# RMSNorm with SiLU: six load buffers as parts of one tile, and four early block loads as two transfers of 64 KB runs

## The chip, the cores and the metric

The kernel runs on one core of one Trainium2 chip. The metric is the device time of one execution in microseconds (us); lower is better. The times shown are medians of several runs; profiles are of one execution each.

## The reference

The input `x` has 8 x 1024 rows of 2048 float32 numbers, `gamma` 2048 numbers, `eps` is 1e-5:

```python
rms = np.sqrt(np.mean(x ** 2, axis=-1, keepdims=True) + eps)
out = gamma * x / rms
return (out * (1 / (1 + np.exp(-out)))).astype(np.float32)
```

Each row is divided by its root mean square, multiplied by gamma, and put through SiLU. 67.1 MB are read and 67.1 MB are written.

## The kernel before, in words

The 8192 rows are cut into 16 blocks of 512 rows. A block is a tile `xt` of 128 partitions, each holding `J = 4` whole rows that lie next to each other in memory: 32 KB per partition, 4.19 MB per block. The pool has six buffers (`BUFS`), so at most six blocks are on the chip, and block b + 6 takes the buffer of block b after that block has been stored. All of the work is done in place.

What each engine does for a block:

- ACT's queue issues the load (`load`, L52 to L55). The queue is also the one that feeds ScalarE with its work, in program order.
- The squares of the four rows are summed, some on ScalarE (`squares_scalar`, L60 to L69, into column j of `ss`), the rest on VectorE (`squares_vector`, L71 to L75). `share(b)` (L77) is the number of rows for ScalarE: 2, or 1 for even blocks from 4 to 12.
- ScalarE takes the root (`root`, L82), VectorE the reciprocal (`invert`, L87), then VectorE multiplies each row by its reciprocal and by gamma (`multiply`, L92, four instructions of 128 x 2048).
- ScalarE applies SiLU in two halves of two rows each (`silu`, L98), and SyncE's queue issues the store (`store`, L102). SyncE issues nothing else apart from gamma's load.
- ScalarE needs another function table for the root than for SiLU: a table load (ACT_TABLE_LOAD, 1.28 us) stands ahead of each root and ahead of the SiLU that follows.

The order on each engine is the order of the program, written out by hand (`manual_schedule`). Loads 0 and 1 are issued at the beginning. Gamma (one row) is copied to all partitions by eight matmuls; ScalarE then copies one element of the result (L116), so that loads 2 to 5 (L117, L118) are issued only after gamma is in place. After that `load(b + 3)` is issued within `squares_scalar(b + 1)`, just after the first square of block b + 1 (L67 to L69), and it waits for the store of the block that had its buffer.

For b below `SOON = 3` and for the last two, a step is: multiply(b), squares_scalar(b + 1), silu(b) with store(b), squares_vector(b + 1), root(b + 1). In between it is: squares_scalar(b + 1), squares_vector(b + 1), root(b + 1), multiply(b), silu(b) with store(b). Then invert(b + 1) follows. The last block is multiplied by gamma alone, and its reciprocal goes into SiLU as a scale, row by row (L152 to L159).

Of the kernel before, what the change touches and what calls it, by code (L numbers as in the profile page):

```python
# [1 line left out]

# [4 lines left out]

ACT = mybir.ActivationFunctionType
ALU = mybir.AluOpType


@with_exitstack
def kernel(
    ctx: ExitStack,
    tc: tile.TileContext,
    x: bass.AP,
    gamma: bass.AP,
    eps: bass.AP,
    out: bass.AP,
):  # L20

    nc = tc.nc
    P = nc.NUM_PARTITIONS
    f32 = mybir.dt.float32
    x2 = x.flatten_outer_dims()
    o2 = out.flatten_outer_dims()  # L30
    n, d = x2.shape
    J = 4
    BUFS = 6
    nblk = n // (P * J)
    xb = x2.rearrange("(b p j) d -> b p (j d)", p=P, j=J)
    ob = o2.rearrange("(b p j) d -> b p (j d)", p=P, j=J)

    singles = ctx.enter_context(tc.tile_pool(name="singles", bufs=1))
    pool = ctx.enter_context(tc.tile_pool(name="pool", bufs=BUFS))
    small = ctx.enter_context(tc.tile_pool(name="small", bufs=2))  # L40
    psum = ctx.enter_context(tc.tile_pool(name="psum", bufs=1, space=bass.MemoryType.PSUM))

    Q = 4
    w = d // Q
    g = singles.tile([P, d], f32)
    eps_t = singles.tile([P, 1], f32)
    ones = singles.tile([P, P], f32)
    junk_a = psum.tile([P, d], f32, name="junk_a")
    junk_v = psum.tile([P, d], f32, name="junk_v")
    blocks, sss, rmss, rstds = {}, {}, {}, {}  # L50

    def load(b):  # L52
        xt = pool.tile([P, J * d], f32, name="xt")
        nc.scalar.dma_start(out=xt, in_=xb[b])  # L54
        blocks[b] = xt  # L55

    def row(b, j):
        return blocks[b][:, j * d:(j + 1) * d]

    def squares_scalar(b, loads=()):  # L60


        sss[b] = small.tile([P, J], f32, name="ss")
        for j in range(share(b)):
            nc.scalar.activation(out=junk_a, in_=row(b, j), func=ACT.Square,  # L65
                                 accum_out=sss[b][:, j:j + 1])
            if j == 0:  # L67
                for s in loads:
                    load(s)  # L69

    def squares_vector(b):  # L71
        for j in range(share(b), J):
            nc.vector.tensor_tensor_reduce(  # L73
                out=junk_v, in0=row(b, j), in1=row(b, j), scale=1.0, scalar=0.0,
                op0=ALU.mult, op1=ALU.add, accum_out=sss[b][:, j:j + 1])  # L75

    def share(b):  # L77
        return 1 if 4 <= b <= 12 and b % 2 == 0 else 2

    def root(b):  # L80
        rms = small.tile([P, J], f32, name="rms")
        nc.scalar.activation(out=rms, in_=sss.pop(b), func=ACT.Sqrt, scale=1.0 / d, bias=eps_t)  # L82
        rmss[b] = rms

    def invert(b):
        rstd = small.tile([P, J], f32, name="rstd")
        nc.vector.reciprocal(out=rstd, in_=rmss.pop(b))  # L87
        rstds[b] = rstd

    def multiply(b):  # L90
        for j in range(J):
            nc.vector.scalar_tensor_tensor(out=row(b, j), in0=row(b, j), scalar=rstds[b][:, j:j + 1],  # L92
                                           in1=g, op0=ALU.mult, op1=ALU.mult)

    def silu(b):
        for h in range(0, J, 2):
            cols = slice(h * d, (h + 2) * d)
            nc.scalar.activation(out=blocks[b][:, cols], in_=blocks[b][:, cols], func=ACT.Silu)  # L98
        store(b)

    def store(b):
        nc.sync.dma_start(out=ob[b], in_=blocks[b])  # L102

    with tc.manual_schedule():

        load(0)
        nc.vector.memset(ones, 1.0)  # L107
        nc.vector.memset(eps_t, float(eps))
        nc.scalar.activation(out=junk_a[:, 0:1], in_=ones[:, 0:1], func=ACT.Square)  # L109
        nc.sync.dma_start(out=g[0:1, :], in_=bass.AP(tensor=gamma.tensor, offset=gamma.offset, ap=[[d, 1], [1, d]]))  # L110
        for c in range(Q):
            cols = slice(c * w, (c + 1) * w)
            nc.tensor.matmul(junk_v[:, cols], ones[0:1, :], g[0:1, cols], start=True, stop=True)  # L113
        load(1)
        nc.vector.tensor_copy(out=g, in_=junk_v)  # L115
        nc.scalar.copy(out=junk_a[:, 0:1], in_=junk_v[:, d - 1:d])  # L116
        for b in range(2, BUFS):  # L117
            load(b)  # L118

        last = nblk - 1
        SOON = 3
        squares_scalar(0)
        squares_vector(0)
        root(0)
        invert(0)
        for b in range(last):
            loads = [b + 3] if BUFS <= b + 3 < nblk else []
            if b < SOON:  # L130
                multiply(b)
                squares_scalar(b + 1, loads)
                silu(b)
                squares_vector(b + 1)
                root(b + 1)
            elif b < last - 1:
                squares_scalar(b + 1, loads)
                squares_vector(b + 1)
                root(b + 1)
                multiply(b)  # L140
                silu(b)
            else:
                multiply(b)
                squares_scalar(b + 1)
                silu(b)
                squares_vector(b + 1)
                root(b + 1)
            if b + 1 < last:
                invert(b + 1)


        for j in range(J):  # L152
            if j == J // 2:
                invert(last)
            nc.vector.tensor_mul(out=row(last, j), in0=row(last, j), in1=g)  # L155
        for j in range(J):
            nc.scalar.activation(out=row(last, j), in_=row(last, j), func=ACT.Silu,  # L157
                                 scale=rstds[last][:, j:j + 1])
        store(last)  # L159


# [1 line left out]
_INS = ['x', 'gamma', 'eps']  # L163
_OUTS = [((8, 1024, 2048), 'float32')]

_NUMBERS = {'eps': 9.999999747378752e-06}


# [26 lines left out]
```

## Time and profile before

| What | Value |
|---|---|
| time, median of 3 runs | 317.02 us (316.7 to 317.08) |
| span of the profiled execution, first to last instruction | 315.1 us (the page gives no time around it; 1.9 us below the median of the runs) |
| VectorE busy | 235.3 us, 75% |
| ScalarE busy | 213.9 us, 68% |
| TensorE busy | 7.2 us, 2% |
| DMA | 134.24 MB, mean 426 GB/s |
| loads | 16 of 4096 KB, median 38.7 us from issue to landing |
| stores | 16 of 4096 KB, median 29.0 us from issue to landing |

How to read it. The page cuts the span into 40 equal slices and gives each engine's busy share of a slice in tenths; DMA is the mean over the core's 16 DMA engines, and the row below it is what they moved in GB/s. A packet is one contiguous run that one DMA engine moves: here 32 KB, a partition's share of a block. A transfer has landed when all of its packets are done and its semaphore has been raised. Loads go through ACT's queue and stores through SyncE's; both are served by the same 16 DMA engines. A line such as "66.72 38.05 DMA xt<-in_x_dram" of the chain of waits is a piece of the chain that ended last: start, length, and what it was. In the timeline an entry has start, length, engine, line, operation, output and inputs, and in brackets how long the engine was idle before and what ended it.

### The profile page before, as it was taken

Reading aid. Unit: us, or ns where it says so; the run is one execution under the profiler, and the core shown is the slowest. Engines: PE = TensorE matmul, PEld = TensorE weight load, DVE = VectorE, ACT = ScalarE, POOL = GpSimd, SP = SyncE. Lnnn points to the kernel's source line nnn. Section 1 sums busy time; section 2 is a strip of 40 time slices with the busy share of each in tenths; the row PEclk is TensorE's granted clock in tenths of the full one; section 3 lists DMA queues with packets and bytes.
Section 4 is the critical chain, followed back from the end, with each engine's and each line's share of the span. In section 5 each row is a group of like instructions: output and inputs, shape, how many; then the busy total and the mean of one; then the engine's idle time right before and its main releaser. Section 6 shows DMA issues by size and latency. Waiting matters only on the chain.

```text
span 315.1 us, 439 instructions
## 1 busy us (share of the span) xinstructions
PE 7.2 (2%) x8; PEld 2.5 (1%) x8; DVE 235.3 (75%) x157; ACT 213.9 (68%) x137; POOL 0.2 (0%) x4
## 2 busy tenths in 40 slices
PE   6200000000000000000000000000000000000000
PEld 2000000000000000000000000000000000000000
DVE  0679697979895695957969489593995939999600
ACT  1269998972799258682687827877278768779910
POOL 0000000000000000000000000000000000000000
DMA  8999999999999999999999999999999999999997
GB/s 334 412 453 416 383 458 408 462 403 462 403 459 408 454 412 458 408 462 403 462 403 462 408 458 408 458 408 458 416 449 416 449 416 449 428 437 428 437 428 308
DMA packets 4613, 134.24 MB, mean 426 GB/s; under 512 B 514, under 2 KB 514, under 8 KB 514
## 3 DMA queue, kind: packets, MB, share of 16 engines
q10 hardware_dynamic: 2304, 67.11, 49.8%
q1 hardware_dynamic: 2306, 67.12, 49.3%
q14 instruction: 3, 0.02, 0.0%
HBM read 67.12 MB, written 67.11 MB: 426 GB/s over the span
## 4 chain that ended last, share of the span: by engine, by line
DMA 68%; DVE 14%; ACT 11%; issue 1%; ACTq 1%; DVEq 0%
DMA xt<-in_x_dram 68%; DVE xt L92 9%; DVE junk_v L73 5%; ACT xt L98 4%; ACT junk_a L65 3%; ACT xt L157 2%; ACT L82 1%; ACTq L190 1%; ACT L157 0%; ACT L98 0%; ACT rms L82 0%; DVE ss L73 0%; ACTq L54 0%; DVE rstd L87 0%; ACT L109 0%
## 5 line engine op out<-in xcount | busy, mean ns | idle before, releaser
L92 DVE SCALAR_TENSOR_TENSOR xt<-xt,rstd,g 128x2048 f32<-128x2048 f32 x60 | 137.0, 2346 | 0.1
L98 ACT ACTIVATE xt<-xt 128x4096 f32<-128x4096 f32 x30 | 108.3, 3615 | 27.4 <-DVE xt L92 27.4
L73 DVE CUSTOM_DVE_ANT_0 junk_v<-xt 128x2048 f32<-128x2048 f32 x37 | 85.1, 2299 | 42.9 <-DMA xt<-in_x_dram 42.2
L65 ACT ACTIVATE junk_a<-xt 128x2048 f32<-128x2048 f32 x27 | 50.7, 1876 | 16.1 <-DMA xt<-in_x_dram 14.0
L82 ACT ACT_TABLE_LOAD x15 | 19.2, 1283 | 26.6 <-DVE ss L73 26.5
L98 ACT ACT_TABLE_LOAD x14 | 18.0, 1283 | 0.2
L115 DVE COPY g<-junk_v 128x2048 f32<-128x2048 f32 x1 | 2.3, 2292 | 9.0 <-PE junk_v L113 9.0
L87 DVE RECIPROCAL rstd<-rms 128x4 f32<-128x4 f32 x16 | 2.7, 172 | 8.4 <-ACT rms L82 8.4
L155 DVE TENSOR_TENSOR xt<-xt,g 128x2048 f32<-128x2048 f32 x4 | 8.9, 2277 | 0.0
L82 ACT ACTIVATE rms<-ss,eps_t 128x4 f32<-128x4 f32 x16 | 4.8, 297 | 5.7 <-DVE ss L73 5.5
L157 ACT ACTIVATE xt<-xt,rstd 128x2048 f32<-128x2048 f32 x4 | 7.7, 1991 | 0.0
L113 PE MATMUL junk_v<-g,ones 1*128 1x512 f32 x8 | 7.2, 1072 | 2.8 <-DMA g<-in_gamma_dram 2.8
L116 ACT COPY junk_a<-junk_v 128x1 f32<-128x1 f32 x1 | 0.1, 144 | 9.8 <-DVE g L115 9.8
L73 DVE DVE_READ_ACCUMULATOR2_ANT ss<- 128x1 f32 x37 | 5.2, 141 | 0.0
L65 ACT ACTIVATION_READ_ACCUMULATOR junk_a<-xt 128x1 f32 x27 | 5.0, 186 | 0.0
L113 PEld LDWEIGHTS junk_v<-g,ones 1*128 1x128 f32 x8 | 2.5, 325 | 5.9 <-issue 5.9
L109 ACT ACT_TABLE_LOAD x1 | 1.3, 1283 | 1.1 <-PEq L176 1.1
L157 ACT ACT_TABLE_LOAD x1 | 1.3, 1283 | 0.0
L107 DVE MEMSET ones<- 128x128 f32 x1 | 0.2, 165 | 0.8 <-PEq L176 0.8
L109 ACT ACTIVATE junk_a<-ones 128x1 f32<-128x1 f32 x1 | 0.2, 174 | 0.0
L176 POOL MEMSET const-bfloat16-1.0<- 128x1 bf16 x1 | 0.1, 103 | 0.0
L176 POOL MEMSET const-uint8-127<- 128x1 uint8 x1 | 0.1, 102 | 0.0
(3 smaller groups left out, 0.3 us busy)
## 6 DMA issues: line engine op xcount, KB each, us to landing
xt<-in_x_dram ACTq DMA_DIRECT2D x16, 4096.0 KB, 38.7
out_dram<-xt SPq DMA_DIRECT2D x16, 4096.0 KB, 29.0
g<-in_gamma_dram SPq DMA_DIRECT2D x1, 8.0 KB
```

Of the source, the lines that this page charges most:

```text
L65: nc.scalar.activation(out=junk_a, in_=row(b, j), func=ACT.Square, accum_out=sss[b][:, j:j + 1])
L73: nc.vector.tensor_tensor_reduce(out=junk_v, in0=row(b, j), in1=row(b, j), scale=1.0, scalar=0.0, op0=ALU.mult, op1=ALU.add, accum_out=sss ...
L82: nc.scalar.activation(out=rms, in_=sss.pop(b), func=ACT.Sqrt, scale=1.0 / d, bias=eps_t)
L87: nc.vector.reciprocal(out=rstd, in_=rmss.pop(b))
L92: nc.vector.scalar_tensor_tensor(out=row(b, j), in0=row(b, j), scalar=rstds[b][:, j:j + 1], in1=g, op0=ALU.mult, op1=ALU.mult)
L98: nc.scalar.activation(out=blocks[b][:, cols], in_=blocks[b][:, cols], func=ACT.Silu)
L109: nc.scalar.activation(out=junk_a[:, 0:1], in_=ones[:, 0:1], func=ACT.Square)
L113: nc.tensor.matmul(junk_v[:, cols], ones[0:1, :], g[0:1, cols], start=True, stop=True)
L115: nc.vector.tensor_copy(out=g, in_=junk_v)
L155: nc.vector.tensor_mul(out=row(last, j), in0=row(last, j), in1=g)
L157: nc.scalar.activation(out=row(last, j), in_=row(last, j), func=ACT.Silu, scale=rstds[last][:, j:j + 1])
L190: with _tile.TileContext(nc) as tc:
```

## The change

The six buffers become one tile, `ring`, of 128 partitions x (6 x 4 x 2048) numbers, in which block b has the part b mod 6. Blocks 2 and 3 are loaded by one transfer, and so are blocks 4 and 5. For that the rows of such a pair lie otherwise over the partitions: each partition takes eight rows that lie next to each other in memory, 64 KB, of which the first four are block 2 (4) and the others block 3 (5). Each of these blocks is still stored by itself, now 32 KB per partition at a step of 64 KB in memory. All else, and the order of the program, is as it was.

```diff
-    xb = x2.rearrange("(b p j) d -> b p (j d)", p=P, j=J)
-    ob = o2.rearrange("(b p j) d -> b p (j d)", p=P, j=J)
+    PAIRS = (2, 4)
+
+    def view(t, b):
+
+        for q in PAIRS:
+            if b in (q, q + 1):
+                both = t[q * P * J:(q + 2) * P * J, :].rearrange("(p j) d -> p (j d)", p=P, j=2 * J)
+                return both[:, (b - q) * J * d:(b - q + 1) * J * d]
+        return t[b * P * J:(b + 1) * P * J, :].rearrange("(p j) d -> p (j d)", p=P, j=J)
...
-    pool = ctx.enter_context(tc.tile_pool(name="pool", bufs=BUFS))
...
-    blocks, sss, rmss, rstds = {}, {}, {}, {}
+    ring = singles.tile([P, BUFS * J * d], f32, name="xt")
+    sss, rmss, rstds = {}, {}, {}
+
+    def rows(b, j, k):
+        at = (b % BUFS) * J + j
+        return ring[:, at * d:(at + k) * d]
+
+    def row(b, j):
+        return rows(b, j, 1)

     def load(b):
-        xt = pool.tile([P, J * d], f32, name="xt")
-        nc.scalar.dma_start(out=xt, in_=xb[b])
-        blocks[b] = xt
-
-    def row(b, j):
-        return blocks[b][:, j * d:(j + 1) * d]
+        nc.scalar.dma_start(out=rows(b, 0, J), in_=view(x2, b))
+
+    def load_pair(b):
+        both = x2[b * P * J:(b + 2) * P * J, :].rearrange("(p j) d -> p (j d)", p=P, j=2 * J)
+        nc.scalar.dma_start(out=rows(b, 0, 2 * J), in_=both)
...
     def silu(b):
         for h in range(0, J, 2):
-            cols = slice(h * d, (h + 2) * d)
-            nc.scalar.activation(out=blocks[b][:, cols], in_=blocks[b][:, cols], func=ACT.Silu)
+            nc.scalar.activation(out=rows(b, h, 2), in_=rows(b, h, 2), func=ACT.Silu)
         store(b)

     def store(b):
-        nc.sync.dma_start(out=ob[b], in_=blocks[b])
+        nc.sync.dma_start(out=view(o2, b), in_=rows(b, 0, J))
...
-        for b in range(2, BUFS):
-            load(b)
+        for b in PAIRS:
+            load_pair(b)
```

## The prediction

> **What bounds the kernel now.** I read the page's slices first, then the busy shares in windows, then the chain of waits, then the landings of the single transfers.
>
> The slices of the page (40 slices of 7.9 us; DMA is the busy share of the 16 DMA engines in tenths):
>
> ```profile
> DVE  0679697979895695957969489593995939999600
> ACT  1269998972799258682687827877278768779910
> ...
> DMA  8999999999999999999999999999999999999997
> GB/s 334 412 453 416 383 458 408 462 403 462 403 459 408 454 412 458 408 462 403 462 403 462 408 458 408 458 408 458 416 449 416 449 416 449 428 437 428 437 428 308
> DMA packets 4613, 134.24 MB, mean 426 GB/s; under 512 B 514, under 2 KB 514, under 8 KB 514
> ```
>
> VectorE and ScalarE have pauses all along; DMA is below nine tenths only in the first and the last slice. The windows make that sharp (the last two columns are the DMA share and GB/s):
>
> ```profile
> 0.00:3.00 3.00, 0.22 (x1) 0.25 (x2) 0.17 (x2) 1.46 (x2) 0.20 (x4) 1.00 0.60 178
> 3.00:10.00 7.00, 6.94 (x8) 2.23 (x8) 0.03 (x1) 0.00 (x0) 0.00 (x0) 1.00 0.99 426
> ...
> 34.00:58.00 24.00, 0.00 (x0) 0.00 (x0) 19.40 (x13) 22.19 (x18) 0.00 (x0) 1.00 1.01 421
> 58.00:96.00 38.00, 0.00 (x0) 0.00 (x0) 35.34 (x25) 27.02 (x18) 0.00 (x0) 1.00 1.01 434
> ...
> 300.00:305.00 5.00, 0.00 (x0) 0.00 (x0) 0.00 (x0) 0.88 (x1) 0.00 (x0) 1.00 1.02 439
> 305.00:313.00 8.00, 0.00 (x0) 0.00 (x0) 0.00 (x0) 0.00 (x0) 0.00 (x0) 1.00 0.98 422
> 313.00:315.00 2.00, 0.00 (x0) 0.00 (x0) 0.00 (x0) 0.00 (x0) 0.00 (x0) 1.00 0.00 0
> ```
>
> From about 2 us to about 313.5 us the DMA engines have no gap at all. One block of 4.19 MB costs them 9.7 us alone: block 0 lands at 12.95 us (issue 0.7 + 12.2), block 1 at 22.7 (1.2 + 21.5), block 2 at 32.4 (12.4 + 20.0). With a load and a store in flight each gets half: a block each in 19.35 us. The chain of waits shows it (start, length, what; two loads in turn take 38.65 us, in which two loads and two stores pass, so 9.66 us each):
>
> ```profile
> 66.72 38.05 DMA xt<-in_x_dram
> 104.77 0.02 issue
> 104.80 0.01 ACT junk_a L65
> 104.80 38.98 DMA xt<-in_x_dram
> 143.78 0.02 issue
> 143.80 0.01 ACT junk_a L65
> 143.81 38.65 DMA xt<-in_x_dram
> ```
>
> So block 0's landing at 12.95 and 31 more blocks (15 loads, 16 stores) of 9.68 us come to 313.0; the last store lands at 314.3 (issued 300.9, 13.4 to landing), and 0.8 us later the span of 315.1 us ends. Only 1.3 us of it is unaccounted for. **The time is the amount of DMA work plus the time in which no transfer is queued.** The change alters neither amount; it can only open a gap or change the rate.
>
> **The change, part by part.**
>
> *Two loads fewer.* ACT's queue issues four transfers at L118 (rows of 0.33 to 0.47 us each, from 12.38 to 14.19) and now issues two. They are queued behind block 1, which is in flight until 22.7, so this is 0. At the engines a queued block costs 9.7 us against 8 packets of 1.21 us, which is 9.68 (128 packets of 32 KB over 16 engines): at most 0.04 us per transfer is the transfer's own. Two fewer: -0.1 us. The Trainium skill, "DMA: Bandwidth & Descriptors", section "Anatomy of one DMA", fits a DMA as about 2.0 us plus its bytes over 436 GB/s; with two DMAs fewer an estimate from it is -4 us. The trace disagrees for queued transfers: 12.95 to 22.7 us is 432 GB/s, with no 2 us in it.
>
> *Blocks 2 and 4 come later.* Now they land at 32.4 and 65.9 us (13.2 + 52.7), blocks 3 and 5 at 46.5 (12.7 + 33.8) and 85.2 (13.7 + 71.5). A pair's semaphore rises when both have landed. No row shows 64 KB runs, so their share beside 32 KB stores is unknown; I bound it. (a) Equal share, as now: pair 2-3 lands at 46.5, where block 3 does. (b) The engines change queue after each run: loads get two thirds. The runs already fetched then also hold back store 0: in the trace its first packet starts at 39.6, 4.4 us after its issue at 35.2, which is 1 us plus nearly three runs of 1.21; with double runs 1 + 2.8 x 2.41 = 7.8, at 43.0. Pair 2-3 then has the engines to itself and lands at 22.7 + 19.4 = 42.
>
> What follows on the engines for (a), with durations of the rows: ACT's two squares of block 2 start at 46.5 instead of 36.7 (4.04 us), the table load of silu 1.28, silu(1) 7.15 us, so store 1 is issued at 59.1 instead of 49.8. Queued behind it on ACT: root(2) 1.6 us until 60.7; VectorE multiplies block 2 from 60.9 to 70.0 (9.14 us); silu(2) and store 2 at 73.7 (now 65.5); squares_vector(3) ends at 74.7, and root(3) at 76.3. Then everything waits for pair 4-5: ACT's square of block 4, and behind it in ACT's queue load 6, whose buffer is free since 58.6 (store 0: 35.2 + 23.4).
>
> When does pair 4-5 land? In (a) it moves 0.62 block until 58.2 beside store 0, then alone until store 1 comes in, 1.0 to 4.4 us after 59.1 (load 0's and store 0's delays): 0.20 to 0.55 block; the remaining 1.18 to 0.83 block at half rate take 22.8 to 16.1 us. So it lands between 83.3 and 80.0 us. In (b) store 1 is issued at 54.7, and at two thirds of 434 GB/s the pair lands at about 70.5; compute reaches the same point, 72 us, at about that time.
>
> *The point that decides: do the engines run dry?* Before load 7 and store 3 are issued, the queues hold loads 0 to 6 and stores 0 to 2, ten blocks whatever the shares. The first lands at 12.95, nine more end at 12.95 + 9 x 9.68 - 0.35 (last byte to landing) = 99.7 us. Load 7 stands in ACT's queue behind silu(3)'s second half, which waits for multiply(3), which stands on VectorE behind three squares of block 4: 0.1 + 7.0 + 9.14 = 16.3 us after the pair, and 1.0 us more to its first byte. So there is no gap if pair 4-5 lands before 99.7 - 17.3 = **82.4 us**. In (b) 12 us are to spare; in (a) 2.4 us are to spare, or 0.9 us are lost. I take 0, since (b) and the slower entry of (a) (the one seen) agree; the bound is 85.2, block 5's landing now, which loses 2.9 us.
>
> After that the gap closes by itself: load 8 follows 14.1 us later (0.2 + two squares 4.8 + 9.1), load 9 16.5 us later, while the two blocks that each step queues last 19.3 us.
>
> *Waits that get tighter.* Load k also waits for store k-6 (load 10 issued at 143.8, store 4 landed at 102.8 + 33.7 = 136.5: 7.3 us to spare). With loads ahead of stores by some 7 us this wait decides, and on ACT the second square, root and silu stand behind it. ACT has 13.4 of 19.4 us per block to do, and the load before still has 8 us or more in the queue: 0, or, if that cover were gone, up to those 7 us once.
>
> *The end.* Load 15 lands at 279.2, and 21.7 us later (300.9) the last store is issued, while store 14 occupies the engines until 304.6. That cover is about 2.4 us. It grows with loads that run ahead, since more stores are left then.
>
> *Strided stores, one tile.* Stores of blocks 2 to 5 write 32 KB runs at a 64 KB step; no row shows that. Nearest rows: the lowest full window is 421 GB/s, the highest 439, against 434. For the eight transfers touched (8 x 9.67 = 77.4 us) that is +2.4 to -0.9 us. I take 0: the 1.21 us of a packet are the same in load-only and mixed windows, so the memory side isn't what limits it. The Trainium skill's same page, section "Latency and other measured facts", speaks against the change: copies between memory tensors with a 512 KiB step per partition are listed at 207 GB/s each way, wider ones lower. At 414 in place of 434 the same eight transfers would cost an estimated +3.7 us; no run here shows such a step.
>
> The ring is one tile, so a wait could be set on more than its own part. Against it: silu(1)'s first half starts at 42.00, when rows 0 and 1 are multiplied (37.01 + 4.6), while the other rows run to 46.15. So waits go by regions of a tile.
>
> ```profile
> 37.01 9.14 DVE L92 SCALAR_TENSOR_TENSOR xt<-xt,rstd,g 128x2048 f32<-128x2048 f32 x4
> ...
> 42.00 3.62 ACT L98 ACTIVATE xt<-xt 128x4096 f32<-128x4096 f32 x1
> ```
>
> **Sum.** Span 315.1 - 0.1 + 0 = 315.0. The page doesn't give what lies around the span; the runs' median of 317.02 is 1.9 above it, so 316.9 us.
>
> **Rivals.**
> 1. *The engines run dry once near 100 us* (slower): pair 4-5 lands after 82.4. For it: the quick entry in (a). Against it: 4.4 us was seen, and (b). Price 0.9 to 2.9 us: 317.8 to 319.8.
> 2. *64 KB runs or 64 KB steps lower the rate* in eight transfers: up to +2.4, 319.3. For it: nothing shows them; against it, the constant packet.
> 3. *More waits than needed*: the store views of blocks 2 and 3 (4 and 5) interleave in memory, so store 3 may wait for store 2's landing and store 5 for store 4's. While a load is queued that is 0; without one it is twice 1.0 + 0.4, or 319.7. If waits went by the whole tile, loads could not overlap compute at all: tens of us.
> 4. *Bigger transfers are faster* (by the 439 GB/s row, -0.9): 316.0. Against it: no gap to close.
> 5. *The change does nothing of the kind*: each 64 KB run is cut into two of 32 KB. That is (a), with the same time.
>
> **Numbers.** Forecast (no change, own range 316.4 to 317.6, with 5 in it) 0.64; rival 1 0.14; rival 2 0.09; rival 3 0.07; rival 4 0.06. 0.2%, or 0.6 us, is about what a measurement of this kernel can tell from no change. So faster 0.06, same 0.64, slower 0.14 + 0.09 + 0.07 = 0.30. The range runs from 316.0 (rival 4) to 319.9 (rival 1's bound), and leaves out the whole-tile waits and worse rates.
>
> **What would show it.** Right: DMA at 9 from the second slice to the last but one, pairs landing at 42 to 47 and 70 to 83 us, store 1 issued 5 to 9 us later, VectorE idle before block 4, and an unchanged span. (b) shows in loads with twice the stores' bytes between 43 and 70 us. Wrong: a slice below 9 near 100 us (rival 1), packets above 1.21 us per 32 KB (2), SyncE waiting on a store's landing (3), or an end where the last store is issued after store 14 has landed.

## The result and the profile after

The kernel with the change takes 317.35 us (median of 21 runs, 316.82 to 317.9), the kernel before 316.96 us (21 runs beside them, 316.7 to 317.31). The ratio is 1.0013, with a 95% interval of 1.0007 to 1.0019: slower by 0.39 us, which is small and clear of the noise. The profiled execution took 317.51 us with a span of 315.7 us, against 315.1 us before; of these two single executions the spans are 0.6 us apart, of the medians 0.39.

The same rows of the page as before, now of the kernel after (busy tenths of 40 slices, then GB/s):

```profile
DVE  0679594497999999979695796947969389997000
ACT  1359629996289968985839558394684996799200
...
DMA  8999999998999999999999999999999999999997
GB/s 333 403 461 432 415 390 423 407 498 369 453 419 445 420 440 428 436 436 432 436 428 461 403 461 403 461 403 461 403 461 403 461 407 457 419 444 419 444 428 307
```

ScalarE has a hole at 39 to 47 us and VectorE one at 47 to 63 us, since block 2 is now awaited longer. DMA reads 9 nearly throughout; the one 8, at 71 to 79 us, has 369 GB/s, and the slice before it 498. There the pair's last 64 KB packets ended and load 6 was issued. A packet is counted whole where it starts: 16 of 64 KB are 1 MB, or 133 GB/s in one slice, so a slice is too coarse to show a loss of half a microsecond. There is no gap near 100 us.

The beginning of the chain of waits after (start, length, what):

```profile
12.33 33.43 DMA xt<-in_x_dram
45.76 0.02 issue
45.78 2.01 ACT junk_a L78 x2
...
51.13 7.12 ACT xt L110 x2
```

The pair 2-3 lands at 45.76, silu(1) starts at 51.13, and store 1 is issued at 58.28 (49.8 before). The pair 4-5 lands at 74.75. What follows on the engines is in the timeline of VectorE and of ACT's queue (ACTq; start, length, engine, line, operation):

```profile
75.73 2.30 DVE L86 CUSTOM_DVE_ANT_0 junk_v<-xt 128x2048 f32<-128x2048 f32 x1
...
82.73 9.13 DVE L105 SCALAR_TENSOR_TENSOR xt<-xt,rstd,g 128x2048 f32<-128x2048 f32 x4
```
```profile
74.78 0.34 ACTq L67 DMA_DIRECT2D xt<-in_x_dram  x1
...
91.91 0.33 ACTq L67 DMA_DIRECT2D xt<-in_x_dram  x1
```

Load 6 goes out as the pair lands, and load 7 at 91.91, 17.2 us after that landing, since VectorE first waits for root(3) and starts its squares of block 4 only at 75.73. Store 3 follows at 95.54. The queues are still full then: load 6 itself lands at 97.77.

The end, in windows (the last two columns are the DMA share and GB/s):

```profile
300.00:305.00 5.00, 0.00 (x0) 0.00 (x0) 0.00 (x0) 0.00 (x0) 0.00 (x0) 1.00 0.97 419
305.00:313.00 8.00, 0.00 (x0) 0.00 (x0) 0.00 (x0) 0.00 (x0) 0.00 (x0) 1.00 1.05 455
313.00:315.00 2.00, 0.00 (x0) 0.00 (x0) 0.00 (x0) 0.00 (x0) 0.00 (x0) 1.00 0.04 16
```

The last store is issued at 294.3, with store 14 in flight until 305.2: 10.9 us of cover, against 3.7 us before (300.9 and 304.6). ScalarE has nothing to do in these windows any more, while before it still worked 0.88 us of the first. Loads run further ahead, and still the end is later.

**Where the 0.4 us come from.** So the loss isn't a gap, nor the end. I summed the packets of the trace: each 32 KB counts 1.21 us of work (64 KB 2.42, the value of undisturbed packets of both kernels), as a mean of the 16 engines. The trace doesn't name a packet's engine; a packet is put to the engine whose packet before it ended just then. Up to 36 us both kernels have done the same. Between 36 and 44 us the kernel after falls 0.56 us behind, and stays there, within 0.1, to the end. In these 8 us the first store comes in beside the loads. Packets of one DMA engine there (L load, S store, start + length in us):

```
before  L33.85+1.21 L35.06+1.21 L36.27+1.90 L38.16+1.62 S39.77+1.21 L40.98+1.21 S42.19+1.21
after   L34.34+2.42 L36.76+2.93 S39.69+1.21 L40.90+3.14 S44.03+1.21 S45.24+1.21 L46.45+2.42
```

Store 0 is issued at 35.2 in both. The load packets in flight while its first packet is brought in take longer: before, two of them by 0.69 and 0.41 us; after, one by 0.51 and another, which follows the first store packet, by 0.72. So it is on ten of the 16 engines after; on the other six the store packet comes later, at 42.5 to 43.0, and the pair's last load packet ahead of it alone is longer by 1.2 to 1.5 us. I call the sum **the entry loss**: a stretch of time around the entry less the work done in it, as a mean of the engines (34.5 to 47 us; shifted where a store was issued later). Before it is 0.86 us, after 1.45: 0.59 apart, as the spans are (0.6).

Not every queue that comes in costs something. In the kernel after, load 6 is issued at 74.78 us, when the last load packets of the pair have ended at 71.5 to 73.2, so its queue is empty, beside running stores. No packet is longer than elsewhere (one engine):

```
after   S69.41+1.21 L70.61+2.42 S73.03+1.21 S74.24+1.21 S75.46+1.21 S76.66+1.21 S77.88+1.21 L79.08+1.21 S80.30+1.21
```

The loss from 72 to 86 us is nothing (under 0.05 us on every engine). So load 6 has no part in the 0.4 us.

### The profile page after: what moved, and what is told of

Its sections match the earlier page's. It is cut to its first block, busy times and chain, and to the rows that moved or that the text cites. A ratio compares the mean times of both kernels' runs of the same rounds, so it can differ in the third digit from the quotient of the medians.

```text
span 315.7 us, 434 instructions
## 1 busy us (share of the span) xinstructions
PE 7.2 (2%) x8; PEld 2.5 (1%) x8; DVE 235.0 (74%) x157; ACT 212.8 (67%) x137; POOL 0.2 (0%) x4
## 4 chain that ended last, share of the span: by engine, by line
DMA 56%; ACT 15%; DVE 15%; issue 3%; PE 2%; ACTq 1%; DVEq 0%
DMA xt<-in_x_dram 31%; DMA out_dram<-xt 25%; DVE xt L105 9%; ACT xt L110 7%; DVE junk_v L86 6%; ACT junk_a L78 3%; PE junk_v L125 2%; ACT xt L169 2%; ACT L95 2%; ACT L110 1%; DVE g L127 1%; ACTq L202 1%; DMA g<-in_gamma_dram 1%; ACT L169 0%; ACT rms L95 0%
## 5 line engine op out<-in xcount | busy, mean ns | idle before, releaser
L110 ACT ACTIVATE xt<-xt 128x4096 f32<-128x4096 f32 x30 | 107.6, 3612 | 15.6 <-DVE xt L105 15.5
L78 ACT ACTIVATE junk_a<-xt 128x2048 f32<-128x2048 f32 x27 | 50.6, 1873 | 30.5 <-DMA out_dram<-xt 15.5
```

Source lines behind the costliest of these rows:

```text
L110: nc.scalar.activation(out=rows(b, h, 2), in_=rows(b, h, 2), func=ACT.Silu)
```

## Experiments

Each was timed beside the kernel before, on the same chip; its median, that of the kernel before and the ratio with its 95% interval are given. The ratio goes by all runs, so where runs lie far apart it differs from that of the two medians. The entry loss is that of its one profiled execution. The runs are called by the beginnings of their names (x1, y4 and so on). The theories named in the expectations:

- **A**: the entry loss grows with the run length of the loads in flight.
- **B**: the layout (one tile, 64 KB steps) costs.
- **C**: 64 KB runs are slow everywhere.
- **D**: each entry of a queue costs, by the entering queue's own runs.
- **E**: the late landing of pair 2-3 and what follows costs.
- **F**: the price is that of a first use of the queue.
- **G**: it is load 6's own entry.
- **H**: it is the end of a load transfer within the entry.
- **P**: it is the phase of the 64 KB packet at which the store comes in.

### The layout alone, one pair alone

The kernel after, with blocks 2 to 5 loaded singly, in the new row order.

```diff
-        for b in PAIRS:
-            load_pair(b)
+        for b in range(2, BUFS):
+            load(b)
```

> The change with its one tile and its interleaved blocks kept, but blocks 2 to 5 loaded one by one (32 KB runs at a 64 KB step). Theory A (the added 0.4 us is lost once, from 36 to 44 us, when the first store comes in beside loads whose runs are 64 KB long): the runs are 32 KB again, so 317.0 us, and the entry of store 0 loses 0.9 us of DMA work as in the kernel before, not 1.5. Rival B (the layout costs: one tile, or stores with 32 KB runs at a 64 KB step): the layout is all there, so 317.35 us. Rival C (64 KB runs are slower wherever they are moved): 317.0 us.

Measured 316.90 us against 316.98, ratio 0.9999 (0.999 to 1.0007), entry loss 0.69. The tile, the changed waits and eight transfers with a 64 KB step in memory cost nothing: B falls.

Only the pair 4-5:

```diff
-    PAIRS = (2, 4)
+    PAIRS = (4,)
...
+        load(2)
+        load(3)
+        load_pair(4)
```

> Only blocks 4 and 5 are a pair; 2 and 3 are loaded one by one. Store 0 comes in at about 36 us beside block 3, which has 32 KB runs. Theory A: 317.0 us, entry loss 0.9 us. Rival B: half of the layout, 317.15 us. Rival C: half of the 64 KB runs, 317.15 us.

Measured 317.06 against 316.98, ratio 1.0018 (1.0002 to 1.0034), entry loss 0.74. The median hardly moves, but three of twelve runs lie at 318.6 to 319.3, where the kernel after has none in 21; the ratio comes from these late runs.

Only the pair 2-3:

```diff
-    PAIRS = (2, 4)
+    PAIRS = (2,)
...
+        load_pair(2)
+        load(4)
+        load(5)
```

> Only blocks 2 and 3 are a pair; 4 and 5 are loaded one by one. Store 0 comes in beside 64 KB runs. Theory A: the whole loss, 317.35 us, entry loss 1.5 us. Rivals B and C: half of it, 317.15 us.

Measured 317.62 against 316.98, ratio 1.0021 (1.0013 to 1.003). Its profile, of its quickest run (317.04), shows an entry loss of 1.13. So the pair 2-3 alone gives at least the whole of the change's loss in time.

Run lengths the other way: before, with block 3, in flight when store 0 comes in, as four loads of 8 KB runs.

```diff
+    def load_by_rows(b):
+        xt = pool.tile([P, J * d], f32, name="xt")
+        blocks[b] = xt
+        for j in range(J):
+            nc.scalar.dma_start(out=row(b, j), in_=xb[b][:, j * d:(j + 1) * d])
...
         for b in range(2, BUFS):
-            load(b)
+            if b == 3:
+                load_by_rows(b)
+            else:
+                load(b)
```

> The kernel before with block 3, the load in flight when store 0 comes in, loaded by four transfers of one row per partition each (8 KB runs). Theory A, if the loss goes with the run length (0.9 us at 32 KB, 1.5 us at 64 KB, by a straight line 0.5 us at 8 KB): entry loss 0.5 us, less some 0.2 us for 24 more packets per engine, so 316.8 us. If the 0.9 us is a fixed price of a first store and only runs over 32 KB add to it: 0.9 us, and 317.2 us with the packets. Rivals B and C say nothing of it: 317.0 to 317.2 us.

Measured 319.47 against 316.98, ratio 1.0107 (1.0073 to 1.014), entry loss 1.11 (in its quickest run, 318.47). So shorter runs in flight don't make the entry cheaper, against A. A further loss adds to the time. With 8 KB against 32 KB a turn, block 3 fell behind the stores, loads stayed late (the last lands at 282.8, 279.2 before), and the last store was issued at 304.52, as store 14 ended. The windows of this kernel:

```profile
295.00:304.00 9.00, 0.00 (x0) 0.00 (x0) 5.09 (x4) 8.96 (x7) 0.00 (x0) 1.00 1.01 437
304.00:306.00 2.00, 0.00 (x0) 0.00 (x0) 0.00 (x0) 0.49 (x1) 0.00 (x0) 1.00 0.65 279
306.00:315.00 9.00, 0.00 (x0) 0.00 (x0) 0.00 (x0) 0.00 (x0) 0.00 (x0) 1.00 0.95 408
```

DMA at 0.65 in the two microseconds after 304 is a short dry stretch: what it looks like when the cover of the end is gone, as the prediction warned.

### Is it a first use, or every entry?

Before, with a small store (512 bytes per partition of `ones`, to a place that the last store writes again) long ahead of store 0, at about 1 us:

```diff
         nc.sync.dma_start(out=g[0:1, :], in_=bass.AP(tensor=gamma.tensor, offset=gamma.offset, ap=[[d, 1], [1, d]]))
+        nc.sync.dma_start(out=ob[nblk - 1][:, 0:P], in_=ones)
```

> The kernel before with one more store of 64 KB (128 runs of 512 B) right at the beginning, into a place that the last store writes again. Theory F (the 0.9 us at 36 to 40 us is the price of the first store ever, paid once): the early store pays it while nothing else is in flight, store 0 comes in for nothing, so 316.1 us. Theory D (each time the store queue goes from empty to full beside loads, the loads slow down while the first store runs are fetched): store 0 pays as before, 0.9 us, so 317.0 us.

and the same beside running loads at 12 us, from `g`:

```diff
         nc.vector.tensor_copy(out=g, in_=junk_v)
+        nc.sync.dma_start(out=ob[nblk - 1][:, 0:P], in_=g[:, 0:P])
```

> The same small store, but issued at about 12.4 us, when loads are in flight. Theory F: the loss of 0.9 us moves from 36 to about 13 us, and the time stays at 317.0 us. Theory D: store 0 still loses its 0.9 us, and the small store adds little, as its run is 512 B: 317.0 to 317.2 us. The trace tells them apart: slow load packets at 13 us alone, or at 36 us still.

Measured 317.20 and 317.22 against 316.85, both ratios 1.0011 (1.0002 to 1.0019). Store 0's entry loss is still there, 0.78 and 0.88, so F falls. And the small store issued at 12 us, whose packets take 0.03 us, slowed no load packet: its entry is free. Both kernels take 0.35 us longer; what takes it isn't shown (the small store's own eight packets per engine are 0.2 us).

Store 0 as four stores of 8 KB runs, in the kernel before and, with the same edit, in the kernel after:

```diff
+        if b == 0:
+            for j in range(J):
+                nc.sync.dma_start(out=ob[b][:, j * d:(j + 1) * d], in_=row(b, j))
+        else:
             nc.sync.dma_start(out=ob[b], in_=blocks[b])
```

> The kernel before with store 0 issued as four stores of one row per partition (8 KB runs). Theory D with a loss that goes with the runs fetched: store 0's first runs are a quarter as long, so the entry loss falls from 0.9 to about 0.3 us, against some 0.2 us for 24 more packets per engine: 316.6 us. If the amount fetched ahead is fixed in bytes, or by theory F: 0.9 us as before and 317.2 us.

> The changed kernel with store 0 issued as four stores of one row per partition (8 KB runs). Theory D with a loss that goes with the store's own runs: entry loss 0.3 to 0.5 us instead of 1.5, so 316.5 us. If the loss goes with the 64 KB runs of the loads in flight, whatever is stored: 1.5 us and 317.5 us.

Measured 317.70 against 316.85, 1.0027 (1.0018 to 1.0036), and 317.35 against 316.85, 1.0021 (1.001 to 1.0032). The entry loss is 0.13 us in both, whatever the run length of the loads:

```
before, by rows  L33.96+1.35 L35.31+1.38 S36.68+0.31 L36.99+1.21 S38.20+0.31 L38.50+1.21
```

So at store 0's entry the price depends on the entering transfer's own runs, as D has it. But no time is won. In the kernel before, 0.9 us go at 84 to 88 us. Store 1, in 32 KB runs, has come in right behind the short ones from 70.5 us and lost nothing; the slow load packets (1.3 to 2.6 us) stand between its last packet and the first one of store 2, which was issued at 65.6. The windows of y4:

```profile
34.00:42.00 8.00, 0.00 (x0) 0.00 (x0) 5.25 (x6) 7.92 (x8) 0.00 (x0) 1.00 1.05 440
84.00:88.00 4.00, 0.00 (x0) 0.00 (x0) 3.97 (x5) 3.43 (x1) 0.00 (x0) 1.00 1.06 360
```

440 GB/s where the kernel before has 393 (36 to 44 us), and then 360. With the change, 0.5 to 0.6 us go at 60 to 64 us, in the last load packet of the pair 4-5. Its profile is of its quickest run (316.96), and its median isn't below that of the change (317.35), so where its other runs lose their time isn't shown.

### Is it the 64 KB run?

The kernel after with the pair 3-4 in place of 2-3 and 4-5: block 2 lands early, and 64 KB runs are in flight when store 0 comes in.

```diff
-    PAIRS = (2, 4)
+    PAIRS = (3,)
...
+        load(2)
+        load_pair(3)
+        load(5)
```

> Blocks 3 and 4 as a pair, 2 and 5 alone. Block 2 lands at 32 us as before, so store 1 is issued at 50 us as before; only what is in flight when store 0 comes in has 64 KB runs. Theory A (run length of the loads in flight at store 0's entry): entry loss 1.1 to 1.5 us and 317.4 to 317.6 us. Theory E (blocks that land later and the later store 1 cost the time): 317.0 us. Theory C (64 KB runs wherever): 317.2 us.

Measured 316.77 against 316.87, ratio 0.9999 (0.999 to 1.0008). Entry loss 0.72, with one engine's packets:

```
pair 3-4  L34.21+2.42 L36.62+3.02 S39.64+1.21 L40.85+2.42 S43.27+1.21 L44.47+2.42
```

The first 64 KB packet takes 0.60 us longer, as in the kernel after (0.51), but the second isn't slowed. So 64 KB runs alone don't cost: A and C fall.

Before, with blocks 2 and 3 and blocks 4 and 5 loaded in swapped order. Block 2 lands as late as in the change by equal shares, with 32 KB runs: E alone.

```diff
-        for b in range(2, BUFS):
+        for b in (3, 2, 5, 4):
             load(b)
```

> The kernel before with its loads of blocks 2 to 5 issued in the order 3, 2, 5, 4: 32 KB runs, but blocks 2 and 4 land where 3 and 5 did (46.5 and 85 us or somewhat earlier), as a pair does. Theory A: entry loss 0.7 to 0.9 us and 317.0 us, as long as the engines don't run dry near 100 us; the prediction's rule says they do not if block 4 lands before 82.4 us, and lose what it is later (at most 2.9 us). Theory E: 317.4 us without a dry spell.

Measured 318.69 against 316.87, ratio 1.0056 (1.0043 to 1.007). Store 0's entry costs 0.71, no more than before. Block 4 lands at 81.47, and the slices of the page show DMA at 9 without a gap, as the prediction's 82.4 us would have it. Yet the median is 1.8 us longer. The profile is of the quickest run (318.06, 1.2 us longer), and its windows and waits tell where:

```profile
84.00:88.00 4.00, 0.00 (x0) 0.00 (x0) 3.97 (x3) 0.00 (x0) 0.00 (x0) 1.00 1.08 410
97.00:101.00 4.00, 0.00 (x0) 0.00 (x0) 3.97 (x5) 3.23 (x1) 0.00 (x0) 1.00 0.97 418
101.00:106.00 5.00, 0.00 (x0) 0.00 (x0) 5.00 (x4) 4.95 (x6) 0.00 (x0) 1.00 1.03 375
```
```profile
ACT junk_a L65 <- DMA xt<-in_x_dram: 21.7, 7, 9.7
```

ACT, behind whose square load 6 stands, waits up to 9.7 us for block 4. The load queue had been empty since 79.6 when load 6 was issued at 81.5: 0.46 us lost by the packets. The store queue had been empty since 96 when store 3 was issued at 101.4: 0.8 us lost, at a DMA share of 1.03. The engines are "busy" while the packets in flight take longer. Together that is this run's 1.2 us: **an entry into a queue that has run empty can cost, even beside a full one**.

It doesn't cost each time, against D. In this same run store 1 was issued at 58.9, with its queue empty since 56.6, and no packet took longer. Load 6 came into an empty queue in the kernel after, in z3, y4, y5, v5 and w2, too, and the mean loss of the engines was under 0.05 us in each. Its transfers have 32 KB runs as in z2, where it cost 0.46, so neither the direction nor the run length tells the costly entries from the free ones; what does is open.

The pair 4-5 alone once more, for its late runs:

> Blocks 4 and 5 as a pair, 2 and 3 alone, for a second time, since its times lay apart (316.6 to 317.1 and 318.6 to 319.3 us). Theory A alone: nothing beyond 317.1 us. Theory G (load 6 comes in beside stores alone, after the pair has left its queue empty, and now and then single DMA engines fall behind there by 1 us or more, which the last store's end then shows): again some runs of 318.5 us and more, and slow packets of load 6 on single engines in the profile.

Measured 317.05 against 316.87, ratio 1.0018 (1.0002 to 1.0034), and again four of eleven runs at 318.5 to 318.9. This profile is of a run of 316.76 us (entry loss 0.76), and load 6 costs nothing in it; that of the first time is of a run of 317.95 us, and two DMA engines lose 0.45 and 0.87 us in it at load 6's first packets there (84 us). The tail's cause stays open.

### What at the entry? Moving it

Store 0 held back to a row boundary of a later block, by a small store ahead of it on its queue that waits for a row of multiply(1); in the kernel before (row 0) and after (row 3):

```diff
         if b > 0:
             store(b)
...
+                if b == 1:
+                    nc.sync.dma_start(out=ob[nblk - 1][:, 0:P], in_=row(1, 0)[:, 0:P])
+                    store(0)
```

> The kernel before (32 KB runs) with store 0 issued some 4.5 us later, behind a 64 KB store that waits for the first row of multiply(1), so that store 0 comes in at 41 to 44 us, just when the load of block 3 ends and that of block 4 begins. Theory H (the entry of a queue costs more when the other queue passes from one transfer to the next within it): entry loss 1.1 to 1.5 us and 317.3 to 317.6 us. Theory A' (only 64 KB runs at such a boundary cost more) or no effect of the boundary: 0.7 to 0.9 us and 317.0 us.

> The changed kernel with store 0 issued behind a 64 KB store that waits for the last row of multiply(1), at about 46.5 us, so that it comes in in the middle of pair 4-5 and not at the end of pair 2-3. Theories H and A': the entry loss falls from 1.45 to 0.7 to 0.9 us and the time from 317.35 to 316.8 to 317.0 us. If 64 KB runs at the first entry cost more wherever it falls: 317.35 us.

Measured 322.04 against 316.89, 1.0155 (1.0142 to 1.0169; a run of 332.73 isn't in the ratio), and 319.70 against 316.89, 1.0088 (1.0075 to 1.0102). These say little on H, for the small store itself was in the way. In the kernel before each of its 8 packets per engine took a turn with a whole load packet, in the kernel after mostly two did, so that store 0 entered only at 51 to 55 us, and at 58 to 62. The entry losses are 0.86 and 1.02. The one with the change then has two more entries that cost: its stores ran dry for 0.6 us at 81, and load 6 (85 to 89 us) and store 3 (105 to 108 us), both into empty queues, cost about 1.3 and 0.7. In the other, the 16 engines drifted apart (their last packets end from 314.8 to 319.0 us), which nothing here explains.

Store 0 held back by other work on ACT instead: two more activations of `g` into the scratch tile ahead of silu(0) in the kernel before, four in the kernel after.

```diff
+        for _ in range(2 if b == 0 else 0):
+            nc.scalar.activation(out=junk_a, in_=g, func=ACT.Silu)
```

> The kernel before with two more SiLUs of gamma (result unused, 2 us each) ahead of silu(0), so that store 0 is issued at 39.2 us without a small store in front of it, and comes in from 40 to 43.5 us, while the load of block 3 (32 KB runs) ends at 41.8 and that of block 4 begins. Theory H (an end of a load transfer within the entry adds to its cost): entry loss 1.1 to 1.5 us in the profile, and 317.3 to 317.6 us. Without such an effect: 0.7 to 0.9 us and 317.0 us.

> The changed kernel with four such SiLUs: store 0 is issued at 43.2 us and comes in from 44 to 48 us, after pair 2-3 has landed at 42 us, within pair 4-5, with 64 KB runs before and behind. Theory H, and any theory that needs the end of pair 2-3: entry loss 0.7 to 0.9 us. If 64 KB runs on both sides are enough: 1.1 to 1.5 us. The whole time may be longer for all theories, since compute is 8 us later and queues may run empty and come in again further on (0.5 to 0.9 us each).

Measured 318.21 against 316.94, 1.0035 (1.0021 to 1.0049), and 318.61 against 316.94, 1.0049 (1.0032 to 1.0067). The first has the end of block 3's load within its entry and loses 0.78; the second enters in the midst of the pair 4-5, where no transfer ends, and loses 1.41. H falls twice. Both take longer than their mean loss says. In the second that is in single engines: two of the 16 lost 2.5 and 2.6 us at the entry (the others 1.1 to 1.4), and these two end last, at 315.4 us by the packets. In the first, profiled in its longest run (319.07), two lost 1.6 and 1.9 us and the last packet ends at 316.1, but whether on one of these two the packets don't tell.

The kernel after, profiled once more for its entry:

> The changed kernel, profiled a second time: whether the entry loss of 1.45 us in its profile, against 0.7 to 0.9 us in the kernels with 32 KB runs, is there again. If it is by chance, 0.7 to 0.9 us here.

317.61 us, entry loss 1.52, and the same pattern of packets (on one engine a load packet of 2.95, then one of 3.17). So the 1.45 repeats.

The pair 3-4 with store 0 some 1 and 2 us later (an activation of half, or all, of a row of `g` ahead of silu(0)):

```diff
+        if b == 0:
+            nc.scalar.activation(out=junk_a[:, 0:d // 2], in_=g[:, 0:d // 2], func=ACT.Silu)
```

> Blocks 3 and 4 as a pair, and one more SiLU over half of gamma (about 1.1 us) ahead of silu(0), so that store 0 is issued some 1.1 us later against the 64 KB runs in flight, each of which takes 2.42 us. Theory P (with 64 KB runs the entry loses between 0.7 and 1.4 us, by where in a run the store arrives): entry loss near 1.4 us where it was 0.72, and 317.4 to 318 us. If the phase doesn't matter: 0.72 us and 316.8 to 317.0 us.

> The same with a SiLU over all of gamma (about 2.0 us), most of a run's 2.42 us. Theory P: the entry loss is nearer to the first again, 0.7 to 1.1 us, or still near 1.4 us if the arrival stays just behind a run's beginning. If the phase doesn't matter: 0.72 us and 316.8 to 317.0 us.

Measured 316.92 and 316.97, both against 316.92: 0.9999 (0.9989 to 1.0008) and 1.0002 (0.9993 to 1.0012), entry losses 0.93 and 0.75 with store 0 issued at 36.30 and 36.93. At the three times tried (35.2 in z1) the loss differs by 0.2 us at most, and none comes near 1.45, so theory P has no support.

| Loads in flight at store 0's entry | Entry loss, us |
|---|---|
| 32 KB runs (before, x1, x2, z3, z2, y1, y2, v4, w2) | 0.69 to 0.88 |
| 64 KB runs of the pair 3-4 (z1, r1, r2) | 0.72 to 0.93 |
| 64 KB runs of the pairs 2-3 or 4-5 (after twice, x3, v5, w3) | 1.02 to 1.52 |
| 8 KB runs (x4) | 1.11 |
| 32 KB and 64 KB runs, store 0 in 8 KB runs (y4, y5) | 0.13, and 0.5 to 0.9 later |

**What is settled and what is open.** The change loses its 0.4 us once, at 36 to 44 us, as store 0 comes in, and the pair 2-3 does it. It isn't the layout, nor 64 KB runs as such, nor a first use, nor a transfer's end in the entry. Nor is it the later landing (E) or load 6 (G): the loss is complete by 44 us, the pair 2-3 lands at 45.76, and load 6 comes in for nothing at 79. Open is why the load packets of pair 2-3 lose 1.45 us at the entry and those of pair 3-4 0.72 to 0.93, why other entries cost nothing, and what the late runs of the pair 4-5 alone are.

## Why the prediction was right and where it failed

*Right.* The time is 0.45 us above the 316.9 forecast and within the forecast's own range, and the difference of 0.13% is under the 0.2% that it took for the least that can be told. But it can be told (1.0007 to 1.0019), and the forecast had nothing there. On the mechanism, (b) held: between 43 and 70 us, the window that the prediction named, loads moved 286 GB/s and stores 148, two thirds to one third, and 64 KB load packets and 32 KB store packets mostly take turns one by one. Pair 4-5 landed 7.7 us ahead of the 82.4 us that decides, so rival 1 didn't come. A 64 KB packet takes 2.418 us where 32 KB take 1.213, and x1's strided transfers cost nothing, so neither half of rival 2 came, nor a gain by bigger transfers (rival 4). Rival 5 falls too: the runs were not cut, the trace has 256 packets of 64 KB. SyncE's waits (line, what ended them: us in total, times, longest) leave out rival 3, for no store (L114) waits for another's landing; L202 is the end of the program:

```profile
SPq L114 <- ACT xt L110: 264.7, 15, 22.5
SPq L202 <- DMA out_dram<-xt: 20.1, 3, 9.6
SPq L114 <- DMA xt<-in_x_dram: 12.0, 1, 12.0
SPq L114 <- ACT xt L169: 10.2, 1, 10.2
```

The wait of load k for store k-6 did come to decide (the largest wait of ACT's squares is now on landing stores, 15.5 us in three), and cost nothing, as the prediction's cover of the queued load had it:

```profile
ACT junk_a L78 <- DMA out_dram<-xt: 15.5, 3, 5.2
ACT junk_a L78 <- DMA xt<-in_x_dram: 14.7, 4, 8.9
```

*Sizes that were off.* In (b) the pair 2-3 was to land at 42 and came at 45.76, where two things were missing. On ten of the 16 engines store 0's first packet started at 39.5 to 39.9, as before, and went ahead of the pair's last one (on the other six it started at 42.5 to 43.0, as predicted); and the entry loss stretched the pair's packets, which ended at 42.5 to 44.2. The landing came 1.6 us behind the last of them, where the prediction had taken 0.35. All dates behind it (store 1 at 54.7, pair 4-5 at 70.5) move by 3.6 and 4.25 us; they are 58.28 and 74.75.

*The step that failed.* "The time is the amount of DMA work plus the time in which no transfer is queued." There is a third term: the work that is lost while store 0 comes in beside the loads. It stood in the rows of before. Of the 1.3 us that the prediction left "unaccounted for", 0.86 are store 0's entry, and the 4.4 us from store 0's issue to its first packet were used to date the landings but priced at nothing. The change moved this term from 0.86 to 1.45 us, which is the +0.6 of the spans. "It can only open a gap or change the rate" was right in words, but the rate was sought in packets away from the entry, where it is constant, and not at the entry. That the missing 0.6 us is small is luck: nothing in the prediction bounded it, and why it grows with the pair 2-3 stays open.

The same missing term would have been worse in the prediction's own scenario (a). Swapping the loads (z2) gave its dates: block 4 at 81.47, within the limit, no dry stretch, and 1.8 us lost. The 82.4 us limit asked when *both* queues are empty; a loss can begin when *one* is, though it needn't (load 6 of the kernel after).

*The two rules that were weighed.* The Trainium skill, "DMA: Bandwidth & Descriptors", section "Anatomy of one DMA", has about 2.0 us per DMA, by a fit to DMAs that GpSimd issues (here ACT and SyncE issue them), which made an estimated -4 us of two transfers fewer. The runs don't show it: x1 issues those two transfers again and is not slower (317.35 with the pairs, 316.90 without). Its section "Latency and other measured facts" made an estimated +3.7 us of the strided transfers by a rate listed for a 512 KiB step. At the 64 KB step here x1 gives 0.9999 (0.999 to 1.0007), which is -0.3 to +0.2 us; no run here has a step of 512 KiB.

## What to carry to other kernels

Where DMA is the bound, "DMA at 9 throughout" doesn't mean that no time is lost: look at the GB/s, and in the trace at single packets, wherever a queue comes in that had been empty. Such an entry cost from nothing to 1.5 us here; the first block store beside the loads, in 32 KB runs, cost 0.7 to 1.5 us in every profile. So keep both queues filled: z2 lost time before the engines ran dry. A longer run also gives a queue a larger share, so look at what becomes of the other queue, and of the last transfer, before runs are lengthened or cut (x4).

## What the runs showed of the hardware

- The 16 DMA engines take turns by packet, not by bytes: 64 KB loads beside 32 KB stores moved 286 against 148 GB/s, and block 3 in 8 KB runs fell behind 32 KB stores (x4). A small packet takes a turn too: 8 per engine, of 512 bytes, held store 0 up until 51 us and more beside 32 KB load packets (w2); beside 64 KB ones mostly two went at a turn (w3).
- Load packets in flight while store 0's first packets come in take longer: 32 KB ones 1.3 to 2.1 in place of 1.21 us (before), 64 KB ones 2.7 to 3.9 in place of 2.42 (after), 8 KB ones some 0.6 in place of 0.31 (x4). With store 0 in 8 KB runs there is next to nothing of it (0.13 us in y4). Later entries into an empty queue cost 0.5 to 1.3 us in z2 and w3 and nothing in others (load 6 after, store 1 in z2).
- Every engine moves its own 8.39 MB, and the slowest sets the end: last packets end at 313.1 to 314.0 us before and 313.7 to 314.5 after. Two instruction fetches of 8 KB, at some 85 to 115 us, cost one engine each 0.4 to 0.7 us before and after (0.31 us of their own, and 0.1 to 0.35 that the store packet behind them takes longer).
